# Rows that arrive transposed, the norm's row factors spread by TensorE, and h sent through memory

## The chip, the cores and the metric

The kernel runs on one core of a Trainium2 chip. The metric is the device time of one execution in microseconds (us), the median of the runs; lower is better. The engines are PE (TensorE, matmuls; PEld is its weight load), DVE (VectorE), ACT (ScalarE), POOL (GpSimd) and SP (SyncE, which here only issues transfers).

## The reference, cut to what matters

One decoder block on 1024 rows of width 1024, in float32:

```python
h = rmsnorm(x, mix_norm_g)              # x * rsqrt(mean(x*x) + EPS) * g, by row
proj = h @ w_in                         # 1024 x 3488
qa, ka, va, q_lat, kv_lat, k_r, g_a, g_b = split(proj)
o_a = swa_sink_attention(rope(qa), rope(ka), va, sinks)    # window 128, 8 heads, 2 kv heads
cq, ckv = rmsnorm(q_lat, q_norm_g), rmsnorm(kv_lat, kv_norm_g)
o_b = mla_attention(cq @ w_uq, ckv @ w_ukv, rope(k_r))     # causal, 8 heads
y = sigmoid(g_a) * (o_a @ w_o_swa) + sigmoid(g_b) * (o_b @ w_o_mla)
x = x + y @ w_out
h = rmsnorm(x, ffn_norm_g)
x = x + (silu(h @ w_gate) * (h @ w_up)) @ w_down
return rmsnorm(x, final_norm_g)
```

## The kernel before

Each float32 product is made of three one-pass products: `split` (L160 to L162) writes the rounded high part on ACT and the rest, "low", on DVE, and `mm3` (L164 to L170) issues high x high, high x low and low x high. The stages follow one another: the projections on blocks of 128 rows, with the local (window) attention interleaved with the gates' products, then the latent attention, the mix and `w_out`, the feed-forward network and the last norm.

The change is almost all in the first of these, and it touches:

- **The rows.** `norm_rows` squares a block on ACT, makes 1/rms on POOL (`rstd_of`, L278 to L282) and multiplies by it and by `g` on DVE (L302). `to_big` turns the block by eight PE transposes (L308) into PSUM and splits it into `quad`, h transposed, four pairs of tiles of high and low. Block 0 alone also comes transposed from the host's layout (`x_t0`), so that its first product can start early.
- **`kvq(b)`** is the product of block b with half of q, with k and with v; `q_first(b)` that with the rest of q; `k_transposes(b)` turns k. Then the `ql` loop makes the latent columns of all blocks, and the `kl` loop the second latent.
- **`set_parts(c)`** prepares for c = 0 to 3 the sums of the four quarters of h that a seven-product scheme (class `Seven`) needs for the gates: `wholes` adds high and low again to h on POOL (four adds), `subs` forms four differences, `splits` three of the splits, and `t4_of_h` the fourth.
- **The local attention's loop**, 16 steps of three gate products (`gate_step`) each, with `sw_qT`, `sw_scores`, `sw_pT`, `sw_pv` between them. `sw_scores` ends on POOL (L775 to L778: the denominators and four scalings); `sw_pT` transposes that on PE. `Seven.mix(j)` makes three sums of the gate weights of column group j on POOL, and a later product a fourth.

PE and SP follow the program's order throughout this part. ACT, DVE and POOL do so only inside two stretches (the first two `kvq`, and the `kl` loop); elsewhere a planner orders them by readiness and the program's order. The pool `u` has 21 slots of 4 KB per partition for all the work tiles, and a transfer on SP waits for a free slot.

## Time and profile before

| | |
|---|---|
| median of 3 runs | 1385.86 us (1385.80 to 1386.17) |
| the profiled execution | 1386.14 us, its span 1384.4 us |
| busy in the span | PE 1350.8 us (98%), PEld 1130.4 (82%), DVE 915.1 (66%), ACT 610.9 (44%), POOL 579.4 (42%) |
| mean granted TensorE clock | 0.994 |

Times inside the profile count from the span's start. The durations of matmuls overlap, so what a matmul costs PE is the distance from its start to the next one's.

### The profile page before, as it was taken

The page shows a single profiled execution, that of the slowest core. Times are in us where ns is not written, and L with a number is a line of the kernel's source. Part 1 is how long each engine was busy: PE and PEld are TensorE (multiplying, and loading weights), DVE is VectorE, ACT ScalarE, POOL GpSimd, SP SyncE. Part 2 cuts the span into 40 slices and gives each one's busy share as a digit, 9 for nine tenths or more (in the row PEclk, how much of TensorE's full clock was granted, in tenths as well). Part 3 has the DMA queues.
Part 4 walks back from the last instruction along what each step waited for, and adds up shares of the span by engine and source line. Part 5 has one row for each costly group of instructions (what it writes and reads, how often), then busy time and mean ns, then how long its engine had stood idle before and what let it go on. Part 6 is the DMA issues. An engine that isn't in the chain of part 4 may idle for free.

```text
span 1384.4 us, 18907 instructions
## 1 busy us (share of the span) xinstructions
PE 1350.8 (98%) x6649; PEld 1130.4 (82%) x6649; DVE 915.1 (66%) x1449; ACT 610.9 (44%) x1214; POOL 579.4 (42%) x590
## 2 busy tenths in 40 slices
PE   8999799999999999999999999999999999999997
PEld 5899688888888887888887788888888888888886
DVE  6757678778767788476348856555666565664763
ACT  5323455654567777563226422323223223644353
POOL 1018754555146565120021556676555652022421
PEclk9999899999999999999999999999999999999999
DMA  5330323323400010473153244453444324997504
GB/s 213 102 102 35 128 73 111 118 96 118 164 1 13 12 62 16 158 268 122 46 213 137 89 171 175 173 202 143 175 160 166 138 100 172 368 371 281 167 2 151
DMA packets 74927, 190.72 MB, mean 138 GB/s; under 512 B 8400, under 2 KB 15056, under 8 KB 74832
## 3 DMA queue, kind: packets, MB, share of 16 engines
q1 hardware_dynamic: 74688, 189.50, 38.4%
q8 instruction: 53, 0.87, 0.2%
q14 instruction: 42, 0.34, 0.1%
q10 hardware_dynamic: 144, 0.00, 0.0%
HBM read 133.90 MB, written 55.57 MB: 137 GB/s over the span
## 4 chain that ended last, share of the span: by engine, by line
PE 74%; DVE 8%; issue 3%; POOL 3%; ACT 3%; DMA 0%; POOLq 0%; ACTq 0%; DVEq 0%; SPq 0%
PE fa L168 7%; PE fa L170 7%; PE fa L169 7%; PE fb L168 5%; PE fb L169 5%; PE fb L170 5%; PE fd L168 5%; PE fd L170 5%; PE fd L169 5%; PE xo L170 2%; PE xo L168 2%; PE xo L169 2%; PE pTb L1025 2%; DVE wl L162 1%; PE oA L170 1%
## 5 line engine op out<-in xcount | busy, mean ns | idle before, releaser
L162 DVE TENSOR_TENSOR wl<-wr,wl 128x512 fp32r<-128x512 f32 x150 | 157.6, 1073 | 73.4 <-ACT wl L161 73.1
L162 DVE TENSOR_TENSOR lrv<-lr,lrv 128x1024 fp32r<-128x1024 f32 x77 | 105.2, 1397 | 49.7 <-ACT lrv L161 45.4
L161 ACT CAST lrv<-lr 128x1024 fp32r<-128x1024 f32 x77 | 80.1, 1052 | 95.5 <-PE fd L170 57.5
L168 PE MATMUL fd<-lrv 128*128 128x512 f32 x308 | 119.8, 389 | 0.0
L169 PE MATMUL fd<-lrv 128*128 128x512 f32 x308 | 119.8, 389 | 0.0
L170 PE MATMUL fd<-lrv 128*128 128x512 f32 x308 | 119.8, 389 | 0.0
L503 POOL TENSOR_TENSOR wr<-wr,sm 128x512 f32<-128x512 f32 x30 | 43.0, 1433 | 129.6 <-DVE wl L162 124.8
L280 POOL TENSOR_SCALAR ms<-ss 128x1 f32<-128x1 f32 x32 | 7.9, 246 | 197.2 <-ACT xn L1397 104.0
L161 ACT CAST wl<-wr 128x512 fp32r<-128x512 f32 x150 | 86.9, 622 | 5.4 <-DMA wr<-in_w_gt_dram 4.6
L162 DVE TENSOR_TENSOR wl<-sm,wl 128x512 fp32r<-128x512 f32 x60 | 48.6, 836 | 37.5 <-ACT wl L161 37.3
L170 PEld LDWEIGHTS fd<-lrv 128*128 128x128 f32 x308 | 57.8, 188 | 12.1
L169 PEld LDWEIGHTS fd<-lrv 128*128 128x128 f32 x308 | 57.8, 188 | 12.0
L168 PEld LDWEIGHTS fd<-lrv 128*128 128x128 f32 x308 | 57.8, 188 | 11.9
L1010 POOL TENSOR_TENSOR denb<-denb,neg_one 128x1 f32<-128x1 f32 x64 | 36.7, 573 | 72.3 <-ACT p L1009 69.0
L1009 ACT ACTIVATE p<-scb,nmb 128x384 f32<-128x384 f32 (+3 forms) x64 | 47.6, 744 | 34.7 <-DVE nmb L1008 33.4
L162 DVE TENSOR_TENSOR ptl<-pTb,pth 128x512 fp32r<-128x512 f32 (+2 forms) x96 | 50.1, 550 | 13.1 <-ACT pth L161 12.9
L1008 DVE CUSTOM_DVE_ANT_0 scb<-scb,mask 128x384 f32<-128x384 f32 (+3 forms) x64 | 48.5, 758 | 13.4 <-PE scb L1000 13.1
L1289 ACT ACTIVATE act<-sm 128x512 f32<-128x512 f32 x11 | 7.0, 633 | 107.0 <-DVE sm L506 107.0
L506 POOL TENSOR_TENSOR sm<-wr,wr 128x512 f32<-128x512 f32 x30 | 40.6, 1353 | 28.7 <-DVE t4l L162 15.2
L1011 POOL TENSOR_SCALAR p<-p,denb 128x384 f32<-128x384 f32 (+3 forms) x64 | 49.8, 778 | 6.3
L773 ACT ACTIVATE pe<-sc,nm 128x256 f32<-128x256 f32 (+1 forms) x64 | 28.8, 458 | 51.3 <-DVE nm L765 51.3
L168 PE MATMUL fb<-t3h,wl 128*128 128x512 f32 x120 | 47.8, 399 | 3.3 <-ACT wl L161 2.1
(335 smaller groups left out, 4348.4 us busy)
## 6 DMA issues: line engine op xcount, KB each, us to landing
lr<-la_d SPq DMA_DIRECT2D x77, 256.0 KB, 5.4
wr<-in_w_gate_dram SPq DMA_DIRECT2D x22, 512.0 KB, 4.1
wr<-in_w_up_dram SPq DMA_DIRECT2D x22, 512.0 KB, 5.0
wd<-in_w_down_dram SPq DMA_DIRECT2D x22, 512.0 KB, 7.0
rb_d<-wd SPq DMA_DIRECT2D x22, 512.0 KB, 2.6
la_d<-sd SPq DMA_DIRECT2D x22, 512.0 KB, 5.4
lr<-rb_d SPq DMA_DIRECT2D x44, 256.0 KB, 5.4
lr<-in_w_down_dram SPq DMA_DIRECT2D x33, 256.0 KB, 5.4
```

Source lines behind the costliest of these rows:

```text
L161: nc.scalar.copy(hi, src)
L162: (eng or nc.vector).tensor_tensor(lo, src, hi.bitcast(F32), op=ALU.subtract)
L168: nc.tensor.matmul(ps, ah, bh, start=first and i == 0, stop=False, skip_group_check=go_on)
L169: nc.tensor.matmul(ps, ah, bl, start=False, stop=False, skip_group_check=go_on)
L170: nc.tensor.matmul(ps, al, bh, start=False, stop=last and i == n - 1, skip_group_check=go_on)
L503: eng.tensor_tensor(out, a, b, op=ALU.subtract)
L506: eng.tensor_tensor(out, a, b, op=ALU.add)
L773: nc.scalar.activation(pe[:, h, c0:], scs[h // 2][:, h % 2, c0:], AF.Exp, scale=SC_A, bias=nm[:, h:h + 1], accum_out=den[:, h:h + 1])
L1008: nc.vector.tensor_tensor_reduce(s_, s_, m_, 1.0, -NEG, op0=ALU.add, op1=ALU.min, accum_out=nm)
L1009: nc.scalar.activation(p_, s_, AF.Exp, scale=-1.0, bias=nm, accum_out=den)
L1010: nc.gpsimd.tensor_tensor(den, den, neg_one[:, 0:1], op=ALU.pow)
L1011: nc.gpsimd.tensor_scalar(p[:, 0:w], p[:, 0:w], den, 0.0, op0=ALU.mult, op1=ALU.add)
```

## The change

- The host's layout gives all blocks transposed (`x_t`), so no block is turned on PE. The untransposed rows are still loaded, for the squares alone.
- `g` goes into the rows of `w_in`: `split_g` scales while it splits, and the gate weights are scaled in place (`scale_gate`, on DVE for j = 0 and on POOL for the others).
- 1/rms of a block is put on a diagonal by POOL; one product with a matrix of ones (`spread`) writes it along the columns of all partitions. `normalize` multiplies the transposed block by it, on POOL for blocks 0 to 4 and on DVE for 5 to 7. Blocks 0 to 4 enter `kvq` without the norm, which is applied to its result (`RAW`); their `quad` is written a second time after `normalize`.
- `h_out` stores the finished h; `load_set` loads it again, in place of `wholes`.
- The order of all five engines is written out from the start to the end of the `kl` loop; there `latent_end` comes one block late, and the first scores of the local attention, the fourth splits and the first gate weights have new places.
- In the feed-forward network's head POOL too follows the program's order, and two preparations come one round earlier.

```diff
+    def split_g(hi, lo, raw, k0):
+        for k in range(raw.shape[1]):
+            g = gT[:, k0 + k:k0 + k + 1]
+            nc.scalar.activation(hi[:, k], raw[:, k], AF.Copy, scale=g)
+            nc.vector.scalar_tensor_tensor(lo[:, k], raw[:, k], g, hi[:, k].bitcast(F32), op0=ALU.mult,
+                                           op1=ALU.subtract)
-            split(hi, lo, raw)
+            if k0 is None:
+                split(hi, lo, raw)
+            else:
+                split_g(hi, lo, raw, k0)
...
-        plain(("x1", j), w_x1[:, 2 * j:2 * j + 2], (P, 2, 512), True)
+        plain(("x1", j), w_x1[:, 2 * j:2 * j + 2], (P, 2, 512), True, 2 * j)
...
-    x_t = U("xt", F32, (P, NK, P))
-    nc.scalar.dma_start(gT, mix_gt)
-    for q in range(2):
-        nc.sync.dma_start(x_t[:, 4 * q:4 * q + 4], x_t0[:, 4 * q:4 * q + 4])
-    st.load_to(1)
-    make_identity(nc, ident)
+    xt = {}
+    rb = {}
+
+    def load_xt(b, pieces=1):
+        xt[b] = U("xt", F32, (P, NK, P))
+        n = NK // pieces
+        for q in range(pieces):
+            nc.sync.dma_start(xt[b][:, n * q:n * q + n], x_t[b][:, n * q:n * q + n])
+            if b == 0:
+                st.load_to(q)
+
+    def load_xs(b):
+        xs[b] = load_x(b)
+
+    dgt = U("dg", F32, (P, 8, P))
+    ones, dg, rbs = dgt[:, 7], dgt[:, 0:4], dgt[:, 4:7]
...
-    xs[1] = load_x(1)
+    nc.scalar.dma_start(gT, mix_gt)
+    nc.scalar.activation(rn[:, 0:1], neg_half, AF.Copy, scale=neg_half)
+    load_xt(0, 2)
     st.load_to(2)
-    g_bc = bcast_gain("mixg", mix_g)
+    load_xt(1)
     st.load_to(3)
+    load_xt(2)
+    load_xs(0)
     ra = U("ra")
     rope_a = ra[:, 0:512].rearrange("p (t b d) -> p t b d", t=2, b=NB)
     nc.sync.dma_start(rope_a, c_rope_a)
-    xs[0] = load_x(0)
-    xs[2] = load_x(2)
-    st.load_to(5)
+    load_xs(1)
+    load_xt(3)
+    make_identity(nc, ident)
...
+    RAW = 5
+
+    def square(b):
+        t = xs.pop(b)
+        sums[b] = tiny("ss")
+        nc.scalar.activation(t, t, AF.Square, accum_out=sums[b])
+        r = rn[:, b:b + 1]
+        rstd_of(sums.pop(b), D, r)
+        nc.gpsimd.tensor_scalar(dg[:, b % 4], ident, r, 0.0, op0=ALU.mult, op1=ALU.add)
+
+    def spread(b):
+        rb[b] = P1("rb", (P, P))
+        nc.tensor.matmul(rb[b], ones, dg[:, b % 4], start=True, stop=True)
+
+    def normalize(b):
+        r, eng = rb.pop(b), nc.vector
+        if b < RAW:
+            nc.scalar.copy(rbs[:, b % 3], r)
+            r, eng = rbs[:, b % 3], nc.gpsimd
+        eng.tensor_tensor(xt[b], xt[b], r.unsqueeze(1).to_broadcast([P, NK, P]), op=ALU.mult)
+
+    def to_quad(b):
+        for q in range(2):
+            hi, lo = quad[(q, b // 4)]
+            split(hi[:, :, blk(b % 4)], lo[:, :, blk(b % 4)], xt[b][:, 4 * q:4 * q + 4])
+
+    def h_out(b):
+        nc.sync.dma_start(h_d[b], xt.pop(b).rearrange("p (a k) c -> p a k c", a=2))
...
+    def k_split(b):
+        pt = kT_ps.pop(b)
         for g in range(NG):
             split(khd[g][0][:, blk(b)], khd[g][1][:, blk(b)], pt[:, g])
...
+    def q_first(b, mid=None):
+        ps = q_ps[b] = P1("qa", (P, 256))
+        pairs = [(hT(k, blk(b)), (wqa[k // 4][0][:, k % 4], wqa[k // 4][1][:, k % 4])) for k in range(NK)]
+        mm3(ps, pairs[:4], last=False)
+        if mid is not None:
+            mid()
+        mm3(ps, pairs[4:], first=False)
...
+    def kvq(b, mid=()):
+
+        mid = list(mid) + [lambda: None] * 2
+        ps = kvq_ps[b] = PX("kvq")
         pairs = [(hT(k, blk(b)), (wx1[k // 2][0][:, k % 2], wx1[k // 2][1][:, k % 2])) for k in range(NK)]
...
+        if b < RAW:
             for k, ((ah, al), (bh, bl)) in enumerate(pairs):
                 nc.tensor.matmul(ps, ah, bh, start=k == 0, stop=False)
+            mid[0]()
             for (ah, al), (bh, bl) in pairs:
...
+                nc.tensor.matmul(ps, al if b == 1 else ah, bh if b == 1 else bl, start=False, stop=False)
+            mid[1]()
             for k, ((ah, al), (bh, bl)) in enumerate(pairs):
...
+                nc.tensor.matmul(ps, ah if b == 1 else al, bl if b == 1 else bh, start=False, stop=k == NK - 1)
         else:
+            mm3(ps, pairs[:3], last=False)
+            mid[0]()
+            mm3(ps, pairs[3:6], first=False, last=False)
+            mid[1]()
             mm3(ps, pairs[6:], first=False)
...
+    by_hand = tc.manual_schedule(engines={engines.Activation, engines.DVE, engines.Pool})
+    by_hand.__enter__()
+    warm = U("warm", BF16, (P, 512))
+    nc.vector.memset(warm, 0.0)
...
+    h0 = U("h0", F32, (P, NK, P))
+    for k in range(NK):
+        if k < 4:
+            nc.scalar.activation(h0[:, k], xt[0][:, k], AF.Copy, scale=gT[:, k:k + 1])
         else:
+            nc.vector.tensor_scalar(h0[:, k], xt[0][:, k], gT[:, k:k + 1], None, op0=ALU.mult)
+    ps = kvq_ps[0] = PX("kvq")
+    for j in range(4):
+        for k in (2 * j, 2 * j + 1):
+            nc.tensor.matmul(ps, h0[:, k], raws[j][:, k % 2], start=k == 0, stop=k == NK - 1)
+        if j < 3:
+            split_g(*wx1[j], raws[j], 2 * j)
+    to_quad(1)
+    split_g(*wx1[3], raws[3], 6)
+    kvq(1)
+    del raws, h0
+    load_xs(2)
+    load_xt(4)
+    load_xs(3)
+    st.load_to(5)
+    to_quad(2)
+    square(0)
+    square(1)
+    kvq(2)
+    load_xt(5)
+    load_xs(5)
+    load_xs(4)
+    load_xt(6)
+    rope_kvq(0)
+    to_quad(3)
+    k_twice(0)
+    rope_kvq(1)
+    to_quad(4)
+    square(2)
+    k_twice(1)
+    kvq(3, (lambda: spread(0), lambda: k_transposes(0)))
+    wqa.extend([halves_of((P, 4, 256), True) for _ in range(2)])
+    split_g(*wqa[0], st.raw.pop(4), 0)
+    normalize(0)
+    rope_kvq(2)
+    split_g(*wqa[1], st.raw.pop(5), 4)
+    st.n_conv = 6
+    square(3)
+    k_split(0)
+    k_twice(2)
+    to_quad(0)
+    kvq(4, (lambda: spread(1), lambda: k_transposes(1)))
+    load_xs(6)
+    h_out(0)
+    normalize(1)
+    rope_kvq(3)
+    square(5)
+    k_twice(3)
+    k_split(1)
+    square(4)
+    to_quad(1)
+    q_first(0, lambda: spread(5))
+    load_xt(7)
+    load_xs(7)
+    normalize(5)
+    rope_q(0)
+    q_first(1, lambda: (k_transposes(2), spread(2)))
+    h_out(1)
+    to_quad(5)
+    normalize(2)
+    rope_kvq(4)
+    square(6)
+    k_split(2)
+    k_twice(4)
+    kvq(5, (lambda: spread(6), lambda: k_transposes(3)))
+    h_out(5)
+    rope_q(1)
+    to_quad(2)
+    normalize(6)
+    k_split(3)
+    q_first(2, lambda: spread(3))
+    h_out(2)
+    st.load_to(st.index[("ql", 0)])
+    rope_kvq(5)
+    to_quad(6)
+    square(7)
+    normalize(3)
+    k_twice(5)
+    kvq(6, (lambda: spread(7), lambda: k_transposes(4)))
+    h_out(6)
+    rope_q(2)
+    k_split(4)
+    normalize(7)
+    to_quad(3)
+    q_first(3, lambda: spread(4))
+    h_out(3)
+    st.load_to(st.index[("ql", 1)])
+    to_quad(7)
+    normalize(4)
+    rope_kvq(6)
+    k_twice(6)
+    st.conv_to(st.index[("ql", 0)])
+    kvq(7, (lambda: None, lambda: k_transposes(5)))
+    h_out(7)
+    nc.sync.dma_start(band, c_band)
+    nc.sync.dma_start(nsink, sinks.partition_broadcast(P))
+    rope_q(3)
+    to_quad(4)
+    k_split(5)
+    q_first(4)
+    h_out(4)
+    st.load_to(st.index[("ql", 2)])
+    rope_kvq(7)
+    k_twice(7)
+    st.conv_to(st.index[("ql", 1)])
+    q_first(5)
+    rope_q(4)
+    k_transposes(6)
+    st.load_to(st.index[("ql", 3)])
+    st.conv_to(st.index[("ql", 2)])
+    k_split(6)
+    q_first(6)
+    rope_q(5)
     nc.vector.tensor_scalar(nsink, nsink, -1.0, None, op0=ALU.mult)
+    st.load_to(st.index[("kl", 1)])
+    q_first(7)
+    rope_q(6)
+    st.conv_to(st.index[("ql", 3)])
+    rope_q(7)
     del wqa
...
+
+    def load_set(c):
+        h_set[c] = [U(n, F32, (P, 2, 4, P)) for n in ("hr", "ht")]
+        for i in range(2):
+            nc.sync.dma_start(h_set[c][i], h_d[c + 4 * i])
+
+    def set_of_h(c, between):
+
...
+        r, t = h_set.pop(c)
...
+        sub(r[:, 0], t[:, 0], r[:, 0], nc.vector)
+        sub(t[:, 0], t[:, 1], t[:, 0], nc.gpsimd)
+        split_h("t1", c, r[:, 0])
+        between()
+        sub(t[:, 1], t[:, 1], r[:, 0], nc.vector)
+        split_h("t3", c, t[:, 0])
+        sub(t4_raw[-1][:, c % 2], r[:, 1], t[:, 1], nc.gpsimd)
+        split_h("t2", c, t[:, 1])
...
+    def latent_end(b):
+        t, ps, r = ql_ps.pop(b)
+        nc.vector.scalar_tensor_tensor(t[:, 0:QL], ps[:, 0:QL], r, qg_bc, op0=ALU.mult, op1=ALU.mult)
...
+        lat_out.append((b, t))
+
+    def lat_store():
+        b, t = lat_out.pop(0)
+        nc.sync.dma_start(lat_d[b][:, 0:C_CKV], t)
...
+            if self.scale is not None and (j, kh) not in self.scaled:
+                self.scaled.add((j, kh))
+                self.scale(j, kh, self.raws[(j, kh)])
...
+    def scale_gate(j, kh, raw):
+        t = raw["g"]
+        for k in range(4):
+            g = gT[:, 4 * kh + k:4 * kh + k + 1]
+            if j == 0:
+                nc.vector.tensor_scalar(t[:, k], t[:, k], g, None, op0=ALU.mult)
+            else:
+                nc.gpsimd.tensor_scalar(t[:, k], t[:, k], g, 0.0, op0=ALU.mult, op1=ALU.add)
...
     for b in range(NB):
-        t = U("lat", F32, (P, C_CKV))
+        if b % 2 == 0:
+            load_set(b // 2)
+        if lat_out:
+            lat_store()
         ps = PX("ql", (P, 416))
         mm3(ps, [(hT(k, blk(b)), (wql[k // 2][0][:, k % 2], wql[k // 2][1][:, k % 2])) for k in range(NK)])
         if b == 0:
             k_transposes(NB - 1)
...
-        if b in (1, 3, 5):
-            sets_of_h(b // 2)
-        if b < 2:
-            wkl.append(st.get(("kl", b)))
-        if b == 6:
-            sw_q(0)
-            sw_q(1)
+            k_split(NB - 1)
+        if b % 2:
+            set_of_h(b // 2, lambda: latent_end(b - 1))
+        elif b:
+            latent_end(b - 1)
+        if b >= 6:
+            wkl.append(st.get(("kl", b - 6)))
+        t = U("lat", F32, (P, C_CKV))
+        ss = tiny("ss")
+        nc.scalar.activation(t[:, 0:QL], ps[:, 0:QL], AF.Square, accum_out=ss)
+        ql_ps[b] = (t, ps, rstd_of(ss, QL))
+    sw_q(0)
+    for kh in range(2):
+        gates.load_part(0, kh)
+    sw_q(1)
     del wql
...
-    by_hand = tc.manual_schedule(engines={engines.Activation, engines.DVE, engines.Pool})
-    by_hand.__enter__()
...
+        if i == 0:
+            latent_end(NB - 1)
+            sw_qT(0)
+            while lat_out:
+                lat_store()
+        if i == 2:
+            gates.prep_to(1)
         if i == 3:
-            parts[1]()
-            gates.prep_to(1)
+            gates.prep_to(2)
         if i == 4:
-            gates.prep_to(2)
+            sw_scores(0)
+        if i >= 4:
+            t4_of_h(i - 4)
         if i == 5:
-            parts[2]()
-        if i == 6:
-            t4_of_h(0)
-            t4_of_h(1)
             gates.mix(0)
-        if i == 7:
-            t4_of_h(2)
-            t4_of_h(3)
         scaled.append((t, r, b))
         if i >= 1:
             kv_out(*scaled.pop(0))
-        if i == 6:
-            sw_qT(0)
     kv_out(*scaled.pop(0))
     gates.prep_to(3)
     by_hand.__exit__(None, None, None)
-    sw_scores(0)
...
-    in_order = tc.manual_schedule(engines={engines.PE, engines.DVE, engines.Activation})
+    in_order = tc.manual_schedule(engines={engines.PE, engines.DVE, engines.Activation, engines.Pool})
...
     for i in range(1, 6):
         if i == 2:
             ffn.prep_to(10)
-        if i == 4:
+        if i == 3:
             ffn.prep_to(12)
         if i == 5:
             ffn.mix(1)
...
-    out = [("x", a["x"]), ("x_t0", tiles(a["x"][0:P].T)), ("mix_g", a["mix_norm_g"]),
+    out = [("x", a["x"]), ("x_t", a["x"].reshape(NB, P, NK, P).transpose(0, 3, 2, 1)),
...
```

216 lines of the change are left out of this document (51 added, 165 removed).

## The prediction

> **What bounds the kernel now.** I read the page first, then the busy time by stretch, then PE's timeline at the places where PE is not full, and last the chain of waits there.
>
> ```profile
> PE 1350.8 (98%) x6649; PEld 1130.4 (82%) x6649; DVE 915.1 (66%) x1449; ACT 610.9 (44%) x1214; POOL 579.4 (42%) x590
> ```
>
> PE is busy for 98% of the span. So only two things count: work taken from PE, and the few stretches in which PE stands. The stretches that the change touches, in the view of windows (busy us of each engine, then the granted clock, the DMA share and GB/s):
>
> ```profile
> 149.30:173.60 24.30, 14.01 (x59) 11.47 (x59) 18.00 (x42) 12.27 (x40) 14.66 (x19) 0.79 0.29 97
> 173.60:345.00 171.40, 170.55 (x866) 142.16 (x867) 133.96 (x309) 93.27 (x259) 89.42 (x117) 1.00 0.31 104
> ...
> 89.20:125.80 36.60, 36.60 (x197) 36.20 (x197) 23.73 (x47) 8.91 (x22) 22.56 (x25) 1.00 0.14 46
> 125.80:149.30 23.50, 23.50 (x196) 23.30 (x194) 15.88 (x31) 9.26 (x28) 20.11 (x24) 1.00 0.33 107
> 18.20:89.20 71.00, 69.90 (x431) 61.42 (x430) 50.51 (x111) 27.66 (x64) 5.21 (x14) 1.00 0.33 107
> ```
>
> From 18.2 to 89.2 (all `kvq` and `q_first`) PE lacks 1.1 us, in the `ql` loop (89.2 to 125.8) and the `kl` loop (to 149.3) nothing, then it stands for 10.3 of 24.3 us at a clock of 0.79, and in the gate loop behind (to 345) it is full again. The hole on PE's timeline, and the chain of waits through it:
>
> ```profile
> 158.21 0.48 PE L757 MATMUL sc<-khd,qs 128*128 128x128 f32 x1 [8.90 <-DVE qs L741]
> ...
> 160.07 0.73 PE L168 MATMUL fa<-hh,wl 128*128 128x512 f32 x1
> ...
> 164.68 0.38 PE L736 MATMUL qT<-ident,qn 128*128 128x128 f32 x2
> 166.02 0.50 PE L168 MATMUL fa<-hh,wl 128*128 128x512 f32 x1 [0.97 <-ACT pu L665]
> ...
> 168.88 0.28 PE L757 MATMUL sc<-khd,qs 128*128 128x256 f32 x1
> ...
> 169.83 0.40 PE L168 MATMUL fb<-t2h,wl 128*128 128x512 f32 x1
> ...
> 172.58 0.60 PE L790 MATMUL pT<-ident,pe 128*128 128x128 f32 x4
> 173.62 0.47 PE L168 MATMUL fb<-t3h,wl 128*128 128x512 f32 x1 [0.44 <-ACT pe L773]
> ```
>
> ```profile
> 139.67 4.51 DMA wr<-in_w_gt_dram
> ...
> 146.83 1.28 POOL ht L503
> 148.13 0.70 DVE ht L503
> 148.90 1.65 POOL h L503
> ...
> 157.43 2.65 POOL wr L503 x2
> ```
>
> PE has finished `kl` at 149.3 and needs `qs`, whose DVE steps stand in a fixed order behind the last set of h. That set is late because POOL first adds high and low together again (`wholes`), and because SP issued the gate weights only at 139.67, behind the latent stores.
>
> **A, the transposes: -5.5 us.**
>
> ```profile
> 50.55 1.03 PE L308 MATMUL tp<-ident,xn 128*128 128x128 f32 x8
> 51.34 0.48 PE L168 MATMUL kvq<-wv,hh 128*128 128x512 f32 x1
> ```
>
> ```profile
> PE tp L308 <- DVE xn L302: 1.1, 3, 0.6
> ```
>
> From start to start, one block's eight transposes cost 0.79 us; eight blocks are 6.3. The 1.1 us that PE waited for `xn` go with them. Against that stand eight `spread` products, which no row shows. They are float32 over 128 columns. The nearest row is the float32 `kvq` of block 0 (below): four entries, two products of 512 columns, in 1.88 us, so 0.235 for 128 columns. A transpose's 0.1 is the lower end, 0.4 the upper; I take 0.235, so 1.9 us. Sum -5.5, bounds -6.6 to -4.2.
>
> **B, the first weights: -2.0 us.**
>
> ```profile
> 15.99 1.04 PE L308 MATMUL tp<-ident,xn 128*128 128x128 f32 x8
> 16.86 1.88 PE L433 MATMUL kvq<-wr,h 128*128 128x512 f32 x4
> 18.18 2.41 PE L438 MATMUL kvq<-wv,hh 128*128 128x512 f32 x8
> ```
>
> ```profile
> 7.73 1.04 ACT L397 CAST wv<-wr 128x1024 fp32r<-128x1024 f32 x1 [1.73 <-DMA wr<-in_w_x_dram]
> ...
> 14.82 1.04 ACT L161 CAST wv<-wr 128x1024 fp32r<-128x1024 f32 x1 [1.93 <-DMA wr<-in_w_x_dram]
> ```
>
> The first weight piece lands at 7.73 with 1.0 MB issued, the fourth at 14.82 with 3.5 MB: 1.42 us for each 512 KB. In the new list the fourth piece ends 3.0 MB, so it lands near 13.4. The last two products (1.88) then end near 15.3, and `kvq(1)` starts there and not at 18.18: 2.9 us, of which block 1's transposes (0.87) stand under A. The splits of that fourth piece are needed only in `kvq(1)`, the low one last, and hide under it; were they late, B would shrink to -0.5.
>
> **C, what covers the front: +3.5 us.** The norm and the splits stay off PE, but DVE gets more to do in less time.
>
> ```profile
> L162 DVE TENSOR_TENSOR hl<-tp,hh 128x512 fp32r<-128x512 f32 x16 | 10.5, 684 | 2.6 <-ACT hh L161 2.5
> L302 DVE SCALAR_TENSOR_TENSOR xn<-x,rstd,mixg 128x1024 f32<-128x1024 f32 x8 | 10.2, 1281 | 5.0 <-DMA mixg<-in_mix_g_dram 2.3 <-POOL rstd L282 1.7 <-ACT hh L161 0.9
> ...
> ```
>
> ```profile
> L506 POOL TENSOR_TENSOR hr<-hh,hl 128x512 f32<-128x512 f32 x8 | 11.6, 1456 | 0.0
> ```
>
> DVE loses eight `xn` (10.2) and gains five more `to_quad` (ten low parts at 0.684: 6.8) and three `normalize` (1.28 each by the `xn` row: 3.8). So 50.5 becomes 50.9 us, in a stretch of about 64 and no longer 71: 80% in place of 71%. ACT, at 27.7 us of 71, gains ten casts and stays off the path. POOL gets five `normalize` of 128x1024; no row has that size, and two of 128x512 at 1.456 give 2.9 each. POOL's work beside DVE's has a price, which two rows of the same small copy show, one alone and one beside a POOL add:
>
> ```profile
> 129.23 1.16 DVE L720 COPY lat<-lat 128x32 f32<-128x32 f32 x1
> ...
> 137.64 0.18 DVE L720 COPY lat<-lat 128x32 f32<-128x32 f32 x1
> ```
>
> A copy of 0.18 us takes 1.16. `to_quad` used to read PSUM; now its low part reads two tiles in SBUF while POOL normalizes. If each `normalize` held DVE for its whole length, that would be 14.5 us against the 13 us that DVE has free, and PE would follow DVE from `kvq(5)` to `kvq(7)`, where each block brings DVE two `to_quad`, a `normalize` and two ropes. If none did, the cost is nothing: what hides it is PE's work, 71 us over eight blocks. I take a quarter, 3.5 us, bounds 0 to 10. The Trainium skill (GPSIMD Engine Reference, section 8, Key points) has a rule that speaks against this step: GpSimd shares its SBUF interfaces with VectorE and collides with DVE instructions that have two SBUF inputs. The two rows agree that something is shared, and applied to every meeting that rule would make C the upper end, and the sum some 6 us higher; how often they meet no row of before shows.
>
> SP now waits inside its list for each `normalize` (`h_out`). Behind the first stand `load_xt(7)`, `load_xs(7)` and the q stores, and behind the third the `ql` weights. They are needed two or more blocks later, at 8 to 9 us per block. The eight stores and loads of h and the seven further transposed blocks raise a DMA share that was 0.33 and 0.14. I price both at nothing; a late `ql` weight would cost its flight, 4 to 5 us by the gate weights' 4.51.
>
> **D, the ql and kl loops: +1.0 us.** `wholes` (four POOL adds per set, 1.456 each) are gone and the sets come from memory one to two blocks ahead. PE keeps its 36.6 and 23.5 us, takes in `sw_scores(0)` (158.21 to 160.07, 1.86 at the low clock; 0.7 taken), and may wait for the last `kl` weights, now split at the very end of `ql` behind the last set: 0.3. Bounds 0.5 and 3.5.
>
> **E, the hole: -12.4 us.** When `kl` ends, the first scores are done, the first gate weights are split (SP issues them before `kl`) and only dense work remains up to the place that was 173.6: three gate products at 2.86 (166.02 to 168.88), 8.6; `qT` and the wait for the copy of the sum, 1.34 (164.68 to 166.02); `sw_scores(1)` 0.95; `sw_pT(0)` 1.04 with its wait. That is 11.9 us in place of 24.3. What is late next is that copy, and it is in the 11.9. Bounds -13.4 (both waits gone) to -5.
>
> **F, the gate loop: +2.5 us.** Each later column group brings eight scalings of 128x256 on POOL.
>
> ```profile
> L778 POOL TENSOR_SCALAR pe<-pe,den 128x256 f32<-128x256 f32 x56 | 31.2, 577 | 1.2
> ...
> L503 POOL TENSOR_TENSOR sm<-sm,wr 128x512 f32<-128x512 f32 x8 | 12.0, 1496 | 0.5
> L506 POOL TENSOR_TENSOR sm<-wr,wr 128x512 f32<-128x512 f32 x8 | 11.7, 1466 | 0.0
> ```
>
> ```profile
> 209.85 2.36 POOL L778 TENSOR_SCALAR pe<-pe,den 128x256 f32<-128x256 f32 x4
> ```
>
> ```profile
> 217.72 1.03 PE L790 MATMUL pT<-ident,pe 128*128 128x128 f32 x8
> ```
>
> The 56 scalings are as many as that row's, 32.3 us at 0.577: POOL goes from 89.4 to 121.7 of 171.4 us, 71%. The probabilities are ready at 212.2 and PE wants them at 217.7, so there are 5.5 us of room. The three sums of a group take 4.4 us together (the third like the two shown), within the room; with the scalings the burst is 9.0. A denominator that meets a whole burst is 3.5 us late. I take one such meeting in seven groups less some part, 2.5 us; bounds 0 and 24.5.
>
> **G, the feed-forward head: -1.5 us.**
>
> ```profile
> 773.62 0.47 PE L168 MATMUL fb<-t3h,wl 128*128 128x512 f32 x1 [2.14 <-ACT wl L161]
> 778.68 0.47 PE L168 MATMUL fb<-t3h,wl 128*128 128x512 f32 x1 [0.70 <-DVE pu L506]
> ```
>
> The 2.14 us are a wait for weights that are now prepared one round earlier; the same DVE and POOL work then stands elsewhere in the same rounds. I take half of the 2.84; bounds -2.8 and, since POOL can no longer pass a waiting step, +1.5.
>
> **The sum.** -5.5 - 2.0 + 3.5 + 1.0 - 12.4 + 2.5 - 1.5 = -14.4 on the profiled execution's 1386.14: 1371.7. The median of the runs lies 0.3 below that execution, so 1371.5.
>
> **The rivals.**
>
> *R1, slower: POOL becomes late in the gate loop.* Place: the denominators and scalings ahead of `sw_pT`. Price: 3.5 us for each of seven groups, F = 24.5, which gives 1393.5. It decides once more than 16.9 us (five of seven bursts) fall on a waiting denominator. For it: PE's order is fixed, so every lateness is PE's; DVE is at 78% there. Against it: the sums can start whenever weights have landed, POOL is free for 29% even then, and PE now waits under 1 us in this loop.
>
> *R2: DVE carries the front.* C at its upper end, 10 us: 1378. For it: the stretched copy and 80% occupancy. Against it: POOL works beside it for only 14.5 of the 64 us, and not all that DVE does in these meets it.
>
> *R3: the hole moves and stays.* The stores of h hold SP, a set or the gate weights come late, or the first sums on POOL, now behind the first softmax, come late: the 8.9 us of idle return elsewhere and the step does not do what it says. 1371.5 + 8.9 = 1380.4. For it: five engines in fixed orders pass a wait on. Against it: POOL loses sixteen adds of some 1.4 us ahead of the hole, which were the late chain.
>
> **How the numbers follow.** The forecast, within 1363 to 1376, gets 0.64; R1 0.10, R2 0.13, R3 0.10; better than all terms 0.03 (C and F at nothing, G whole: 1364, so hardly under 1362). What a measurement of this kernel can tell from no change is about 0.2%, 2.8 us. Faster by more: the forecast, R2, most of R3, the better case, 0.87. Slower by more: R1, 0.10. Between them 0.03. The range reaches from 1362 to 1382: it takes in R2 and R3 and leaves out R1.
>
> **What would show it.** In the new profile: no `tp` from `xn`, `kvq(1)` starting near 15.3; the first `ql` product near 85.2 and not 89.2 (near 82 would put C at nothing; a DVE at over 90% from 45 to 65 would speak for R2); `kl` ending near 146; no wait of over 2 us at the first gate product, and the clock at 1.00 there; in the gate loop waits of `pT` for POOL under 3 us in sum. The forecast is wrong if PE's waits for DVE before the `ql` loop exceed 10 us, if the hole is still over 5 us, or if POOL's scalings precede waits of `pT` in most groups.

## The result, and the profile after

The change made the kernel slower: 1390.99 us (median; 1388.52 to 1391.54) against 1386.60 for the kernel before, a ratio of 1.0029 with a 95% interval of 1.0019 to 1.0039. The profiled execution's span is 1388.5 us, 4.1 above the 1384.4 before. The prediction had 1371.5 (1362 to 1382), so 18.5 us of its own sum have to be found. Ratios below are to runs of the kernel before on the same chip in turn, because its median moved from 1384.9 to 1387.0 between the groups of runs.

The busy times of the page after, and the view of windows with the prediction's stages (busy us by engine, then the granted clock, the DMA share, GB/s):

```profile
PE 1347.6 (97%) x6600; PEld 1124.8 (81%) x6600; DVE 922.9 (66%) x1481; ACT 621.1 (45%) x1248; POOL 600.9 (43%) x643
```

```profile
18.20:85.00 66.80, 62.75 (x372) 53.98 (x371) 56.49 (x120) 32.26 (x82) 22.71 (x25) 1.00 0.57 201
85.00:121.50 36.50, 36.50 (x196) 36.12 (x195) 23.00 (x53) 10.93 (x28) 13.88 (x18) 1.00 0.58 197
121.50:156.60 35.10, 27.23 (x203) 26.45 (x203) 22.03 (x61) 15.45 (x49) 14.04 (x26) 0.85 0.23 77
156.60:170.40 13.80, 10.85 (x53) 8.31 (x51) 9.50 (x20) 6.59 (x20) 7.07 (x10) 1.00 0.41 128
170.40:342.60 172.20, 168.57 (x853) 139.29 (x853) 134.77 (x304) 90.90 (x256) 117.05 (x173) 1.00 0.31 103
```

PE has 3.2 us less to do and a span 4.1 us longer. The `ql` loop now starts at 85.0 (89.4 before) and is full. The `kl` loop behind it, which took 23.5 us without a gap, takes 35.1: PE is busy for 27.2 of them, and the clock is 0.85. The stretch that was the hole (24.3 us) is down to 13.8. In the gate loop PE lacks 3.6 us, where it lacked 0.9.

What PE waited for (us in sum, times, longest), from 18 to 85, in the `kl` loop, from 157 to 345, and in the feed-forward head (`wh` and `wl` are the high and low part of a weight, `hl` the low part of h, `dg` the diagonal, `qs` the split q, `ptl` the low part of the transposed probabilities, `pu` a product taken out of PSUM or a sum of two):

```profile
PE rb L402 <- POOL dg L398: 1.9, 2, 1.8
PE qa L169 <- DVE hl L161: 1.3, 2, 1.0
PE kvq L169 <- DVE hl L161: 0.6, 1, 0.6
...
PE kl L167 <- ACT wh L215: 4.9, 1, 4.9
PE kl L168 <- DVE wl L216: 3.0, 2, 2.0
...
PE sc L889 <- DVE qs L873: 3.1, 5, 2.0
PE fa L167 <- DVE ptl L161: 1.3, 1, 1.3
PE fb L169 <- DVE wl L161: 1.0, 2, 0.5
...
PE fb L167 <- DVE pu L625: 3.8, 1, 3.8
```

The largest is new: the `kl` weights, 7.9 us. The timeline shows how it comes about (start, duration, in brackets the idle time before and its releaser):

```profile
84.88 2.91 SPq L442 DMA_DIRECT2D q_d<-qn  x2
...
89.37 0.38 SPq L643 DMA_DIRECT2D hr<-h_d  x1
89.79 0.43 SPq L643 DMA_DIRECT2D ht<-h_d  x1
...
97.11 0.69 DVE L622 TENSOR_TENSOR hr<-ht,hr 128x512 f32<-128x512 f32 x1 [5.92 <-DMA ht<-h_d]
105.81 0.68 DVE L622 TENSOR_TENSOR hr<-ht,hr 128x512 f32<-128x512 f32 x1
114.52 0.69 DVE L622 TENSOR_TENSOR hr<-ht,hr 128x512 f32<-128x512 f32 x1
119.99 1.70 ACT L215 ACTIVATE wh<-wr,gT 128x256 fp32r<-128x256 f32 x4
123.75 0.39 PE L168 MATMUL kl<-wl,hh 128*128 128x256 f32 x1 [1.95 <-DVE wl L216]
124.80 0.68 DVE L622 TENSOR_TENSOR hr<-ht,hr 128x512 f32<-128x512 f32 x1
129.76 1.70 ACT L215 ACTIVATE wh<-wr,gT 128x256 fp32r<-128x256 f32 x4
130.32 0.58 PE L167 MATMUL kl<-wh,hh 128*128 128x256 f32 x1 [4.88 <-ACT wh L215]
131.93 0.58 PE L168 MATMUL kl<-wl,hh 128*128 128x256 f32 x1 [1.04 <-DVE wl L216]
```

SP's list has the first set of h behind the last q stores, and these wait for DVE's ropes (84.88, with its wait 2.91). So the set is asked for at 89.4 and DVE, idle for 5.9 us, starts on it at 97.1. From there ACT, DVE and POOL hand each other the steps of a set in 8.7 us (97.11, 105.81, 114.52), while PE needs 9.1 for its two blocks (36.5 us for eight): hardly anything is caught up. The `kl` weights are split behind the third and behind the fourth set, at 120.0 and 129.8, and PE, which could have started both by 122, waits for each. The first product behind the long wait then runs at half clock (0.58 against 0.28), and the clock stays at 0.50 until 136.

The balance, by the starts of the same products in both traces:

| stage | predicted | measured |
|---|---|---|
| A + B + C, to the first `ql` product (89.4 to 85.0) | -4.0 | -4.4 |
| D, to the end of `kl` (149.3 to 156.6) | +1.0 | +11.7 |
| E, to the first `fb<-t3h` product (173.62 to 170.36) | -12.4 | -10.6 |
| F, to the last `pT` (341.8 to 342.6) | +2.5 | +4.1 |
| G, the feed-forward head | -1.5 | +2.0 |
| the rest (latent attention 0.7, tail 0.6) | 0 | +1.3 |
| sum | -14.4 | +4.1 |

Of the 18.5 us between the two sums, D is 10.7, G 3.5, E 1.8, F 1.6 and the rest 1.3, and the front is 0.4 better than forecast.

### The profile page after: what moved, and what is told of

It reads as the page before. It is cut to its first block, busy times and chain, and to the rows that moved or that the text cites. A ratio compares the mean times of both kernels' runs of the same rounds, so it can differ in the third digit from the quotient of the medians.

```text
span 1388.5 us, 18957 instructions
## 1 busy us (share of the span) xinstructions
PE 1347.6 (97%) x6600; PEld 1124.8 (81%) x6600; DVE 922.9 (66%) x1481; ACT 621.1 (45%) x1248; POOL 600.9 (43%) x643
## 4 chain that ended last, share of the span: by engine, by line
PE 77%; DVE 7%; issue 4%; POOL 3%; ACT 3%; DMA 1%; SPq 0%; POOLq 0%; ACTq 0%; DVEq 0%
PE fa L169 7%; PE fa L167 7%; PE fa L168 7%; PE fb L167 5%; PE fb L168 5%; PE fb L169 5%; PE fd L169 5%; PE fd L167 5%; PE fd L168 5%; PE xo L167 2%; PE xo L169 2%; PE xo L168 2%; PE pTb L1148 2%; PE oA L167 1%; PE oA L169 1%
## 5 line engine op out<-in xcount | busy, mean ns | idle before, releaser
L161 DVE TENSOR_TENSOR wl<-wr,wl 128x512 fp32r<-128x512 f32 x150 | 153.0, 1043 | 78.7 <-ACT wl L160 78.4
L1133 POOL TENSOR_TENSOR denb<-denb,neg_one 128x1 f32<-128x1 f32 x64 | 36.5, 570 | 72.9 <-ACT p L1132 69.5
L168 PEld LDWEIGHTS fd<-lrv 128*128 128x128 f32 x308 | 57.8, 188 | 12.4 <-DVE lrv L161 0.3
L1131 DVE CUSTOM_DVE_ANT_0 scb<-scb,mask 128x384 f32<-128x384 f32 (+3 forms) x64 | 48.4, 757 | 13.4 <-PE scb L1123 13.1
```

Of the source, the lines that this page charges most:

```text
L161: (eng or nc.vector).tensor_tensor(lo, src, hi.bitcast(F32), op=ALU.subtract)
L168: nc.tensor.matmul(ps, ah, bl, start=False, stop=False, skip_group_check=go_on)
L1131: nc.vector.tensor_tensor_reduce(s_, s_, m_, 1.0, -NEG, op0=ALU.add, op1=ALU.min, accum_out=nm)
L1133: nc.gpsimd.tensor_tensor(den, den, neg_one[:, 0:1], op=ALU.pow)
```

## The experiments

The diffs are against the changed kernel ("after"), cut to the edit.

### The kl weights and the sets of h

Theory T1: late hand-overs of the kind above, each with its own place, ate the gain. Its rival T2: PE has no slack left, and what is won at one place is given back at the next.

**e1**, the `kl` weights split at blocks 0 and 1 of the `ql` loop:

```diff
-        if b >= 6:
-            wkl.append(st.get(("kl", b - 6)))
+        if b < 2:
+            wkl.append(st.get(("kl", b)))
```

> Only edit to the changed kernel: the two weight pieces of the second latent are split at blocks 0 and 1 of the ql loop instead of 6 and 7. Theory T1 (the weights' split stands in ACT's and DVE's fixed order behind the last set of h, and that is what PE waits for, 7.9 us in three waits and then a cold clock): the waits at the first kl products vanish, the kl loop ends 9 to 11 us earlier, and the whole takes 1380 to 1383 us. Rival T2 (ACT and DVE are behind as such, so what they owe comes due at the next consumer, qs, the kl copies or the first gate products): the kl wait moves there, and at most 4 us are won, 1387 to 1390.

Measured: 1384.39 us, ratio 0.9986 (0.9977 to 0.9995), 6.6 us under the changed kernel by the medians and 6.0 by the ratios. T1 had 1380 to 1383, so most of its gain came and not all. `kl` ends at 148.8 and not 156.6, and all of that is still there at the output projection (its first product at 641.2, 648.9 in after). One edit of two lines takes the kernel from slower to slightly faster. What PE waits for in the `kl` loop now is a single load, so a part of the wait did move on, as T2 had it:

```profile
PE qT L868 <- DMA qn<-q_d: 2.8, 1, 2.8
```

**e2**, the first set asked for ahead of the last q stores:

```diff
+    load_set(0)
     st.load_to(st.index[("kl", 1)])
     q_first(7)
 ...
-        if b % 2 == 0:
+        if b % 2 == 0 and b > 0:
             load_set(b // 2)
```

> Only edit: the first set of h is loaded ahead of the kl weights and the last two q stores (about 5 us earlier in SP's list), instead of at the start of the ql loop. Theory T1 with the memory as its origin (DVE stood 5.9 us for the first set's flight at the loop's start and the lateness is carried through four sets of 8.7 us each): the sets start about 5 us earlier, the wait at the kl weights falls from 7.9 to about 3 us, the whole takes 1384 to 1387. Rival (the sets are paced by PE's ql products, so the flight is made up before the kl loop anyway): no change, 1390 to 1392.

Measured: 1385.78 us, ratio 0.9996 (0.9987 to 1.0005). DVE starts on the first set 6 us earlier, and the waits for the `kl` weights shrink from 7.9 to 3.3 (DVE's timeline, PE's waits):

```profile
91.06 0.68 DVE L630 TENSOR_TENSOR hr<-ht,hr 128x512 f32<-128x512 f32 x1
...
PE kl L167 <- ACT wh L215: 2.1, 1, 2.1
PE kl L168 <- DVE wl L216: 1.2, 1, 1.2
```

So both ends of the chain are shown: the late load (e2) and the place of the weights behind it (e1). T1 holds here for most of the loss.

### The gate loop

**e3** leaves out the gains of gate groups 1 to 7:

```diff
-            else:
-                nc.gpsimd.tensor_scalar(t[:, k], t[:, k], g, 0.0, op0=ALU.mult, op1=ALU.add)
```

> Leaves out the factor g of the gate weights for column groups 1 to 7 (the 56 scalings on POOL), so the gates there lack it. Theory (step F: the scalings make POOL late in the gate loop, which took 4.1 us more than before from the first t3 product to the last transposes): 3 to 4 us come back, 1387 to 1388. Rival (the loop lost them to DVE and ACT in an order that the planner changed, or to POOL holding DVE): 0 to 1 us, 1390 to 1391.

Measured: 1387.36 us, ratio 1.0006 (0.9997 to 1.0015), 3.6 under after. From the third to the last `qT` the loop takes 147.6 us, 151.0 in after and 147.0 before: 3.4 of F's 4.1 are the scalings. The waits that go are small ones for DVE (157 to 345):

```profile
PE sc L887 <- DVE qs L871: 2.4, 3, 2.0
...
PE fa L167 <- DVE ptl L161: 0.4, 1, 0.4
```

What makes DVE late shows in the softmax's two smallest steps, `nm` and `es`. They take 0.16 us each, and in e3 all of them do. In after, with the scalings ahead of them, POOL's three sums fall into the softmax (some scalings too), and a step that meets one of these operations ends with it, as here (POOL's and DVE's timeline, after):

```profile
179.65 1.29 POOL L622 TENSOR_TENSOR sm<-sm,wr 128x512 f32<-128x512 f32 x1
179.94 1.02 DVE L897 SCALAR_TENSOR_TENSOR nm<-mx,nsink 128x4 f32<-128x4 f32 x1
```

Over the 16 steps of the loop `nm` and `es` together take 6.0 us more than at 0.16 each.

**e7** is e1 with these scalings on ACT; **e7s** is e1 with them on POOL, but away from the three sums:

```diff
-                nc.gpsimd.tensor_scalar(t[:, k], t[:, k], g, 0.0, op0=ALU.mult, op1=ALU.add)
+                nc.scalar.activation(t[:, k], t[:, k], AF.Copy, scale=g)
```

> e1, and the gains of gate groups 1 to 7 multiplied in by ACT in place of POOL. T1 (the gate loop loses 3.4 us because POOL's scalings lie ahead of its three sums): those 3.4 us are back, 1381 by e1's 1384.4. T2 (the loop has no room for 56 more operations on any engine: ACT's bursts of eight at 0.47 us delay copies and exponentials that PE waits for): no gain, 1384 to 1388.

> e1, and the scalings left on POOL but taken out of the burst: those of a group's first half at its second product before, those of the second half two products later, and the sums of the next group two products earlier. T1 (the burst is the cost): at least half of the 3.4 us come back, 1381 to 1383 by e1's 1384.4. T2 (what counts is that DVE's operations are stretched whenever POOL works, wherever that is): no gain, 1384 to 1385.

Measured: 1381.25 (ratio 0.9965, 0.9953 to 0.9978) and 1383.08 (0.9969, 0.9958 to 0.9981), against e1's 0.9986. The same stretch of the loop takes 148.8 and 149.5 us (151.0 in e1). ACT gives back 2.2 of the 3.4, spreading 1.4; the excess of `nm` and `es` falls with them, from 6.0 us to 0.8 in e7 and 2.5 in e7s. So the place of POOL's burst is part of the cost. e7 keeps 1.2 of the 3.4; what ACT's scalings delay was not followed. The two medians alone could not tell e7 from e7s.

### The front

**e6** leaves out the multiplication of blocks 0 to 4 by their row factors; **e11** does it on DVE:

```diff
         if b < RAW:
-            nc.scalar.copy(rbs[:, b % 3], r)
-            r, eng = rbs[:, b % 3], nc.gpsimd
+            return          # e6; in e11: pass
```

> The changed kernel without the multiplication by the row factors of blocks 0 to 4 (the five POOL operations of 128x1024 and the copies ahead of them are left out; those blocks go on unscaled); nothing else differs. T1 (the prediction's term C: POOL's norm beside DVE's splits costs the front about 3.5 us): the 3.8 us in which PE waited for dg and hl go, the first ql product moves from 85.0 to about 81.5, and the time falls by 3 to 4 us from 1391.0, to 1387 to 1388. T2 (DVE has too much work in the front whatever POOL does): the first ql product stays at 84 to 85 and the time at 1390 to 1391.

> The changed kernel with the norm of blocks 0 to 4 on DVE, as for blocks 5 to 7, and not on POOL. DVE gets five operations of about 1.28 us more, 6.4 in all. T1 (the front loses 4.7 us, as e6 measured, because POOL's norm stretches DVE's splits and holds up dg behind it): the first ql product moves from 85.0 to 82 to 83, and the time falls by 2 to 4 us from 1391. T2 (DVE has no room for 6.4 us more in the front): the first ql product comes at 85 to 88 and the time is 1391 to 1394.

Measured: e6 1383.48 (ratio 0.9982, 0.9974 to 0.9991), first `ql` product at 80.3; e11 1388.94 (1.0028, 1.0017 to 1.0039), at 83.5. The norm of these blocks costs the front 4.7 us. e6's whole gain is 7.5 us (6.5 by the ratios), more than T1's 3 to 4; the part behind the front was not followed. DVE does the norm for 3.2, so moving it gains 1.5, less than T1 had, and by the ratio nothing that can be told from after: at the first `fb<-t3h` product the two are level (170.15, 170.36 in after). How POOL costs DVE time is in the group of `hl` (min/median/max in ns), after and e6:

```profile
L161 DVE TENSOR_TENSOR hl<-xt,hh x20: 678/683/2885, 19.7 to 73.3; 128x512 fp32r<-128x512 f32 x20
```

```profile
L161 DVE TENSOR_TENSOR hl<-xt,hh x20: 679/682/691, 19.8 to 67.2; 128x512 fp32r<-128x512 f32 x20
```

One split that met a `normalize` of 2.62 us on POOL took 2.885 in place of 0.68; without POOL's norm none took over 0.69. A rope step of 0.28 us took 2.48 beside another `normalize` (58.32). The rule of the Trainium skill that the prediction weighed (GPSIMD Engine Reference, section 8, Key points) holds for these rows, but few operations meet it: the front lost half of what the upper end had.

### The feed-forward head

**e4** undoes both edits there, **e4b** only the preparation:

```diff
-    in_order = tc.manual_schedule(engines={engines.PE, engines.DVE, engines.Activation, engines.Pool})
+    in_order = tc.manual_schedule(engines={engines.PE, engines.DVE, engines.Activation})   # e4 only
 ...
-        if i == 3:
+        if i == 4:
             ffn.prep_to(12)
```

> Undoes the two edits in the feed-forward head alone: POOL is free of the program's order there again, and the two preparations come one round later, as before. Theory (step G had the wrong sign: POOL in fixed order keeps DVE's adds back, PE waits 3.8 us for them): about 2 to 3 us come back, 1388 to 1389, with waits of 2.1 and 0.7 us as before. Rival (that stretch depends on what comes before it and not on these edits): no change, 1391.

> The changed kernel with the feed-forward weights prepared up to the twelfth in round 4 again, and POOL still in the written order. T1 (the earlier preparation puts two splits ahead of the sum that PE waits for, and POOL's order costs the rest, 0.7 us ahead of the output projection): the head's waits for wl and pu become 2.1 and 2.1 in place of 0.8 and 3.8, and the time falls by about 0.5 us from 1391, to 1390 to 1391. T2 (POOL's order costs nothing, the earlier preparation all that e4 gave back): 1389 to 1389.5.

Measured: e4 1389.16 (ratio 1.0019, 1.0010 to 1.0029), e4b 1390.22 (1.0033, 1.0020 to 1.0045). The times do not tell them apart from after, but the traces do: both wait 2.1 for `wl`, as before, and then 2.1 for `pu`, and their heads are equally long within 0.1 us, so POOL's order costs nothing there. Yet e4's head (from the first product of the output projection to the last `fb<-t3h`) is still 1.6 us longer than before the change (2.0 in after). What differs is where the clock was low. The product that waited 2.1 us for `wl` and the one behind it, before and in e4:

```profile
774.85 0.57 PE L170 MATMUL fb<-t3h,wl 128*128 128x512 f32 x1
...
777.36 0.63 PE L170 MATMUL fb<-t3h,wl 128*128 128x512 f32 x1
778.68 0.47 PE L168 MATMUL fb<-t3h,wl 128*128 128x512 f32 x1 [0.70 <-DVE pu L506]
```

```profile
775.12 0.47 PE L167 MATMUL fb<-t3h,wl 128*128 128x512 f32 x1 [2.14 <-ACT wl L160]
...
777.72 0.39 PE L169 MATMUL fb<-t3h,wl 128*128 128x512 f32 x1
780.18 0.71 PE L167 MATMUL fb<-t3h,wl 128*128 128x512 f32 x1 [2.08 <-DVE pu L625]
...
782.83 0.63 PE L167 MATMUL fb<-t3h,wl 128*128 128x512 f32 x1
783.67 0.39 PE L169 MATMUL fb<-t3h,wl 128*128 128x512 f32 x1
```

From wait to wait both take 5.06 us. Before, half clock (0.63 us a matmul) came 1.2 us into the first product and lay under the wait for `pu`, where it cost nothing. In e4 the first product ran at full clock, waited 2.1 us, and the second ran slow, on PE's path. This slow stretch lasts about 3.4 us (780.18 to some 783.6). The Trainium skill (TensorE: Matmul & The Clock Gate, Part 1) has the clock follow a free-running window of 3413 ns; the length agrees, and a window that runs freely would explain why the same waits meet it differently, which the runs here do not prove.

**e14** puts nine unread products ahead of the second wait (in e10, below):

```diff
+        if ffn.seq[ffn.n_run] == (0, 7, "u"):
+            ps = P1("fill")
+            for _ in range(9):
+                nc.tensor.matmul(ps, w7[:, 0, 3], hq["b11"][0][:, 0], start=True, stop=True)
         j, q, m = ffn.run()
```

> e10, with nine products of 128x512 on TensorE whose result nobody reads, put ahead of the product that waits 2.1 us for the sum in the feed-forward head. T1 (the head costs 1.6 us more than before the change because the stretch of half clock of 3.4 us, which before the change lay under a wait, now lies under products): the clock stays full behind the wait, the product there takes 2.8 and not 4.4 us, the head's excess of 1.6 us goes and the time falls by 1 to 2 us, to about 1375.2. T2 (the head is slower for another reason): no gain, 1376.5 to 1378.

Measured: 1376.60 us (ratio 0.9925, 0.9912 to 0.9937) against e10's 1376.70 (0.9938, 0.9924 to 0.9951). In its profile the head's excess of 1.6 us is gone and the clock stays full:

```profile
765.46 2.20 PE L1569 MATMUL fill<-b11h,wl 128*128 128x512 f32 x9
767.73 0.47 PE L167 MATMUL fb<-t3h,wl 128*128 128x512 f32 x1
```

But the profile of e13, without the fill, has no excess either (the slow stretch fell under the wait again), and that of e15, with it, has 1.3 us (the clock was low ahead of the fill, 0.63 us a matmul). So the place of the slow stretch is what the head gains or loses, shown in the traces; that the fill pays is not shown.

### One lateness that moves

**e5** (e1, and the local q rows loaded at block 6), **e9** (e5, POOL's first three sums ahead of the first softmax), **e10** (e9 with e7's and e4's edits):

```diff
+        if b == 6:
+            sw_q(0)                     # e5; taken out behind the loop
 ...
         if i == 4:
+            gates.mix(0)                # e9; taken out at i == 5
             sw_scores(0)
```

> The kl weights split at blocks 0 and 1 of the ql loop, as in e1, and besides the load of the first local q rows issued at block 6 and not behind the loop. T1 (the loss in the ql and kl loops is late hand-overs, each with its own place): the 2.8 us that the first qT waited for q_d in e1 go, kl ends near 146 and not near 149, and the time falls by 2 to 2.8 us from e1's 1384.4, to 1381.6 to 1382.4. T2 (PE is paced there by what DVE and ACT do together, and the wait only had that name): qT then waits for another engine and the time stays within 1 us of 1384.4.

> e5, and POOL's first three weight sums for the gates issued ahead of the first softmax and not behind it. In e5 PE waited 3.3 us for the copy of the first gate product, which stands on ACT behind a split that waits for the first of these sums. T1 (the wait that e5 took from qT came back there, because POOL does the sums last): the 3.3 us fall under 1 us, and the time falls by 2 to 3 us from e5's 1383.0, to 1380 to 1381. T2 (the softmax, now late on POOL, is the next to be waited for): PE waits for the probabilities or the scores in place of the copy, and the time stays at 1382 to 1384.

> e9 with the scalings of the gate weights on ACT (as in e7) and the feed-forward head as before (as in e4). T1 (the losses are separate hand-overs and add up): e9's time less 2 to 3 for the scalings and 1 to 2 for the head, 1376 to 1378. T2 (each time that PE gets ahead it meets another late engine): 1379 to 1382.

Measured: e5 1383.01 (ratio 0.9974, 0.9965 to 0.9983), e9 1380.65 (0.9959, 0.9946 to 0.9971), e10 1376.70 (0.9938, 0.9924 to 0.9951). e10 is where T1 had it, and e9's time too, but not by the way that T1 had. e5 ended `kl` at 146.9 as expected, and then PE waited 3.3 us for a copy on ACT; e9 was to cure that, and the wait stayed at 3.25. **e13** splits the first gate weights a block earlier and makes the sums right behind them; **e17** (on e15, below) puts the first scores two blocks earlier and the gate weights back where after has them:

```diff
-        if i == 2:
+        if i == 1:
             gates.prep_to(1)
-        if i == 3:
+        if i == 2:
             gates.prep_to(2)
+            gates.mix(0)                # taken out at i == 5
```

```diff
         if i == 2:
+            sw_scores(0)                # e17; taken out at i == 4, where gates.mix(0) goes
             gates.prep_to(1)
```

> e10, with the first two gate weights split one kl block earlier (after the second and third block) and POOL's first three sums put right behind them, ahead of the first softmax and of the later kl factors. In e9 the copy that PE waits for stood behind a square on ACT, and that behind POOL's kl factors, which followed 9 us of sums and softmax in one piece. T1 (it is POOL's one long piece, which no exchange within it could cure): the 2.8 us of waiting that e10 still has at the second gate product fall under 1 us and the time falls by 2 to 3 us from e10's 1376.7, to 1374 to 1375. T2 (the hand-over from the kl loop to the gates is bound by ACT and DVE together): another wait of 2 us or more stands there and the time stays at 1376 to 1377.

> e15, with the first scores and their softmax two kl blocks earlier (after the third block, ahead of the first gate weights) and POOL's three sums after the fifth. In e13 the sums were early and PE still waited 3.8 us for the copy on ACT: ACT stood 4.1 us before the exponentials, for DVE, and then had four latent copies and squares and four splits of t4 to do one after the other before the copy. T1 (ACT's queue behind the first softmax is what keeps the hole): the wait falls under 1 us and the time falls by 2 to 3 us, from e15's 1375.7 to 1373. T2 (another of the engines' queues takes its place, as after e5, e9 and e13): a wait of 2 us or more stands there again and the time stays within 1 us of 1375.7.

Measured: e13 1376.81 (0.9931, 0.9917 to 0.9944), e17 1376.55 (0.9927, 0.9913 to 0.9940). T1 fell in both: the wait was 3.8 and 3.7. One row each of e5, e9, e13 and e17 shows who was late:

```profile
152.14 0.62 ACT L160 CAST wl<-sm 128x512 fp32r<-128x512 f32 x1 [2.25 <-POOL sm L622]
153.30 0.80 PE L167 MATMUL fa<-hh,wl 128*128 128x512 f32 x1 [3.26 <-ACT pu L783]
```

```profile
150.94 0.42 ACT L958 ACTIVATE lat<-lat 128x256 f32<-128x256 f32 x1 [2.76 <-POOL ms L293]
```

```profile
144.84 0.37 ACT L906 ACTIVATE pe<-sc,nm 128x128 f32<-128x128 f32 x1 [4.06 <-DVE nm L898]
```

```profile
133.67 0.48 PE L889 MATMUL sc<-khd,qs 128*128 128x128 f32 x1 [3.69 <-DVE qs L873]
```

In e5 the copy stands on ACT behind a split that waits for POOL's sum; in e9 behind a square that waits for POOL's row factors; in e13 ACT waited 4.06 us for DVE ahead of the exponentials; in e17 PE waits for DVE in the `kl` loop itself. PE's own wait is for the same copy in the first three, but what holds it up is another operation each time, and the length is 3 to 4 us in all four. That suggests that the three engines are late as a group when they leave the sets; the next runs test it.

**e16** is e13 with e11's norm, **e15** that with e14's fill, and **e18** is e15 with e2's early load.

> e13 with the norm of blocks 0 to 4 on DVE (as in e11). T1 (what e11 gained in the front, 1.5 us at the first ql product, is PE's and is not given back): e13's time less 1.5 to 2, 1372.5 to 1373.5. T2 (the front's gain is lost at the sets of h, which wait for DVE): e13's time unchanged.

> e16 and e14 together: all the hand-overs mended. T1 (the losses add up): e16's time less the 1 to 2 us of e14, 1371 to 1372, which is about what the prediction had for the change itself. T2 (they do not): 1373 to 1376.

> e15 with the first set of h loaded ahead of the last q stores, as in e2. T1 (the waits of 3 to 4 us that wandered from the kl weights to qT, to the copy and to the first scores in e1, e5, e9, e13 and e17 are one lateness: the sets of h start 5 to 6 us late because their first load does, and ACT, DVE and POOL carry that through all that follows): the first set starts near 91 and not at 96.2, the wait for the copy (3.7 us in e15) falls under 1 us, and the time falls by 2 to 3 us from e15's 1375.7, to 1373. T2 (the three engines have more work between 120 and 155 than PE, whenever the sets begin): the wait stays at 3 us or more and the time within 1 us of 1375.7.

Measured: e16 1375.61 (0.9924, 0.9912 to 0.9937), e15 1375.72 (0.9919, 0.9905 to 0.9933), e18 1371.90 (0.9894, 0.9877 to 0.9910). e16 and e15 are not to be told from e13, so the repairs do not add up here (T2 in both). e18 is 3.8 us under e15 (3.5 by the ratios). DVE's first step of a set in both traces, then PE in e18's:

```profile
96.22 0.69 DVE L621 TENSOR_TENSOR hr<-ht,hr 128x512 f32<-128x512 f32 x1 [4.11 <-DMA ht<-h_d]
```

```profile
93.39 0.68 DVE L629 TENSOR_TENSOR hr<-ht,hr 128x512 f32<-128x512 f32 x1
...
149.28 0.50 PE L167 MATMUL fa<-hh,wl 128*128 128x512 f32 x1 [1.50 <-ACT pu L783]
```

The set starts 2.8 us earlier (not the 5 expected), now without a wait for the load, and the wait for the copy falls from 3.7 to 1.5 (T1 had under 1). Behind e15's longer wait PE also ran at half clock (0.63 us a matmul from 153.3, 0.40 in e18), so e18 is 3.5 us ahead at the first `fb<-t3h` product. At the output projection 1.5 of them are left; what the rest went to was not followed. So the late first load accounts for 2.2 of the 3.7, and curing its victims one by one had moved that wait and not shortened it. Whether the other 1.5 is the engines' own work, as T2 had it, stays open. e18 is 1.1% faster than the kernel before and the fastest kernel here.

## Why the prediction was wrong, point by point

**A, B and C** (-4.0 predicted, -4.4 measured) came out right in sum with two errors that cancel. `kvq(1)` starts at 13.30 and not 15.3:

```profile
11.91 1.95 PE L503 MATMUL kvq<-wr,h 128*128 128x512 f32 x4 [0.22 <-DMA wr<-in_w_x_dram]
13.30 2.42 PE L451 MATMUL kvq<-wv,hh 128*128 128x512 f32 x8
```

The last products of block 0 could start at 11.91, when the fourth weight piece was in, and not at 13.4: the prediction took the pace of the loads from before, and they came faster. So B was worth about 4.0 and not 2.0. C is then 5.1 by subtraction (with A as predicted), and 4.7 by e6 for POOL's norm alone, against 3.5 taken. DVE is busy for 56.5 us in this stretch and not for 50.9; in e6 it is 50.2, so the excess is what POOL's norm does to it. Not DVE alone was late: the longest wait there is POOL's, 1.8 us for `dg`, which stands behind a `normalize` in POOL's order. A was not measured by itself.

**D is the step that failed.** It said that the sets "come from memory one to two blocks ahead" and that PE "may wait for the last `kl` weights, now split at the very end of `ql` behind the last set: 0.3". The wait was named and its price was not worked out: 7.9 us, and by subtraction some 3 more for half clock behind it (the loop's excess of 11.6 less the 7.9, and less the 0.9 that the scores and transposes cost in e1). To price it, the sets' own path had to be followed: asked for behind two q stores that wait for DVE, landed 7 to 8 us later, 8.7 us each, four of them. That comes out at 132, ten us after PE wants the weights; 89.4 and 97.1 could not be read off the trace of before, but the list on SP and the order on ACT could be read in the code.

**R3** named this mechanism ("a set or the gate weights come late") at a chance of 0.10, with the 8.9 us of the old hole as its price: the hole would move and undo E. The lateness struck the `kl` loop, and E kept most of its gain besides, so the sum became D +10.7 over its term and not E undone.

**E** (-12.4, measured -10.6) was right, and not only because a late `kl` gave the other engines time: in e1, where `kl` ends 7.8 us earlier, the stretch is as short (148.8 to 162.7). One wait of 2.0 us is left at the first gate products, for DVE's `qs`.

**F** (+2.5, measured +4.1) had the right cause, the scalings (3.4 by e3), and the wrong way: PE never waits for POOL's probabilities. POOL's burst holds DVE's `nm` and `es` (6.0 us over the loop), DVE's splits come late behind them, and PE waits for these.

**G** (-1.5, measured +2.0 in the head) had the wrong sign, and most of the 2.0 is not the edits': e4, without them, still loses 1.6 to the place of the half clock, which in after too lies under products (0.63 us each from 781.8). The edits' own share is some 0.4 (waits of 0.84 and 3.75, 2.14 and 2.08 in e4). The wait for `wl` went from 2.1 to 0.8, as said, but "the same DVE and POOL work then stands elsewhere" hid the cost: two splits come ahead of the sum that PE needs next, stretched by POOL's adds beside them (DVE's and POOL's timeline, after):

```profile
776.50 3.42 DVE L161 TENSOR_TENSOR wl<-sm,wl 128x512 fp32r<-128x512 f32 x2
...
777.67 1.71 POOL L622 TENSOR_TENSOR wr<-wr 128x512 f32<-128x512 f32 x1
779.85 0.68 DVE L625 TENSOR_TENSOR pu<-fb,pu 128x512 f32<-128x512 f32 x1
```

Such a split takes 0.68 alone later in this head (782.13), and the two take 3.42 here; PE waits 3.75 for the sum. Another 0.7 us was lost in the latent attention and 0.6 in the tail, neither of them in the prediction; neither was followed further.

**R1 and R2** did not happen: the gate loop lost 4.1 and not 24.5 us, and the front's cost stayed at half of its upper end.

## What to carry to other kernels

When a step is moved behind another in a fixed order, follow the chain that feeds that other from the queue that issues its load, and count its steps to the time at which the moved result is wanted; a wait that can be named can be priced. When a wait that is taken away comes back with another releaser and the same length, look upstream for the one late start that all of them inherit. Whether the repairs that showed nothing by themselves (e13, e14, e16) add to what the mended start gave is not shown: e10 with the early load alone was not run.

## What the hardware showed that was not expected

- A DVE operation with both inputs in SBUF is held by the POOL operation that it meets, however small it is: `nm`, 0.16 us alone, took 1.02 and ended at 180.96, with POOL's sum (180.94). In a row of them 0.68 us becomes 1.71 beside POOL's adds of 1.71 (two in 3.42, above), and 2.885 beside a `normalize`.
- Half clock does not follow a wait at once. After waits of 2.1 us it came 1.2 us into the next product or only behind the next wait, lasted 3.4 us, and cost 0 or 1.6 us for the same first wait.
